# Spreading c by a VectorE shuffle instead of a TensorE product, with x squared on other engines

## The chip, the core and the metric

One core of a Trainium2 chip runs the whole program; seven cores are idle. The metric is the device time of one execution in microseconds (us), lower is better. The kernel before took 355.51 us (median of three runs, 355.11 to 355.52).

## What is computed

One layer of a hybrid model on 256 tokens of width 1024: an adaptive norm of x, a wide projection, block attention, a chunked mLSTM, a gated sum and an output projection. Only its head matters here:

```python
ada = c @ w_ada + b_ada
shift, scale, gate = jnp.split(ada[:, None, :], 3, axis=-1)
h = _rmsnorm(x, norm_w) * (1 + scale) + shift
... = jnp.split(h @ w_in, SPLIT_IDX, axis=-1)
```

c is one row of 1024 numbers. Every channel of `shift` and `scale` is a dot product of c with one column of w_ada, and `_rmsnorm` divides each token by the root of the mean of its squares plus 1e-6.

## The kernel before, in words

TensorE (PE) needs the normed, modulated x transposed, channels on the partitions: eight tiles k = 0 to 7 of 128 channels by 256 tokens, each kept as a high part `hTh` and a low part `hTl`, since every product is made from two-part numbers in three passes. The first projection phase ("P1", lines 186 and around) multiplies them with eight slabs of `w_row`, each split into `wrh` and `wrl` by ScalarE (ACT) and VectorE (DVE). After it some 25 chunks of 512 columns go through TensorE in a ring, with attention and mLSTM work hooked in between.

The order of the work on each engine is the order of the program (a manual schedule); within P1 it is a written list of steps, `P1_STEPS`, each a letter and a number. An engine takes its instructions strictly in that order, so an instruction that waits holds up all behind it. Loads go out on two queues: SyncE's (SP) carries x in two halves, then the slabs of w_ada (`adat`) and of `w_row` by turns; ACT's own queue carries c, the small table `params` (`prm`) and the bias table `relT`.

What stands ahead of P1, the part that the change touches:

- **c to all partitions (`cb`, 128 x 1024).** c lands in one partition (`crow`, a view of the second half of `xnT`, free until the transposed x is put there). Line 224 multiplies a row of ones with it, two products of 512 columns on PE into PSUM (`pc`), and line 227 on DVE and 228 on ACT copy the two halves into `cb`. `cb` is one operand of every dot product with w_ada (step `C0`, line 138, on DVE: `Ab` and `Bb`, the scale and shift of tile 0).
- **Squares and roots.** Half t of x (`xt`, 128 tokens by 1024) is squared and summed into `ssx`: half 0 on ACT (line 225), half 1 on DVE (line 229). `rstd(t)` on GpSimd (POOL) adds epsilon (line 205) and takes the power -1/2 (line 206) into `rsx`. ACT scales a unit matrix by it into `diag` (line 233).
- **Transposes with the norm in them.** `T0`, `T1`, `T2` (line 243) multiply 128 x 128 blocks of x with `diag`, so that PSUM receives normed x transposed (`xps`). A transpose of the pair kp holds four such products, two of half 0 and two of half 1. Step `t0` (line 248, ACT) copies the first pair into `xnT`.
- **Modulation.** Step `w0` (line 170, ACT) rounds the first slab, step `H0` (lines 158 and 162, ACT) makes `hTh` and `hf` of tile 0 from `xnT`, `Ab` and `Bb`; DVE makes `wrl` (line 175) and `hTl` (line 165). Step `P0` (line 186) is the first product of P1.
- **Dummies.** `keep_clock(n)` (line 217) issues n products of the unit matrix with itself into a bank that nobody reads: two at the start (`WARM = 2`), five after the products with c (step `K5`). In the trace each 128 x 128 product of this type is two records.

POOL fills the bias table (`rel_prep`, line 268) after the roots.

Of the kernel before, what the change touches and what calls it, by code (L numbers as in the profile page):

```python
# [9 lines left out]
F32 = mybir.dt.float32  # L10
F32R = mybir.dt.float32r
AF = mybir.ActivationFunctionType
OP = mybir.AluOpType
AX = mybir.AxisListType

D = 1024
# [4 lines left out]
EPS = 1e-6  # L21
# [17 lines left out]

P1_STEPS = ("R0 R1 R2 R3 K5 T0 t0 T1 T2 C0 w0 U0 H0 G0 B0 P0 x0 z0 y0 t2 B1 t1 L1 c1 a1 w1 k1 v0 Q0 q0 n0 T3 m0 "
            + "".join(f"b{k} i{k} U{k} j{k} G{k} x{k} " + ("t3 " if k == 2 else "") + f"L2 c{k + 1} z{k} y{k} a{k + 1} "
                      f"w{k + 1} k{k + 1} v{k} e{k} " for k in range(1, 7))
            + "b7 i7 U7 j7 G7 x7 z7 y7 v7 P7 Q7 q7 N7 M7").split()
WARM = 2

KX = 248
NR = 1536 + KX + 8
# [15 lines left out]
def tile_hybrid(ctx: ExitStack, tc: tile.TileContext, x, c, params, params2, rel_t, w_row, ada_mod, ada_gate,  # L65
                w_in, w_att_proj, w_ml_proj, w_out, out):
    nc = tc.nc
# [15 lines left out]
    ident = consts.tile([128, 128], F32, name="ident")  # L83
    ones = consts.tile([128, 128], F32, name="ones")
# [9 lines left out]
    mhalf = consts.tile([128, 16], F32, name="mhalf")  # L94
    qns = consts.tile([128, 1], F32, name="qns")
    ssx = consts.tile([128, 2], F32, name="ssx")
    rsx = consts.tile([128, 2], F32, name="rsx")
# [5 lines left out]
    pp = p1.enter_context(tc.tile_pool(name="ps1", bufs=1, space=PS))  # L103

    xt = ph.tile([128, 2, D], F32, name="xt")
    xnT = ph.tile([128, KT, S], F32, name="xnT")

    for t in range(2):
        nc.sync.dma_start(xt[:, t], x2[:, t])
    crow = xnT[0:1, 4:8].rearrange("p k s -> p (k s)")  # L110
    nc.scalar.dma_start(crow, c)
    nc.scalar.dma_start(prm, params)
    nc.scalar.dma_start(relT, rel_t)
    make_identity(nc, ident)
    nc.vector.memset(ones, 1.0)
# [26 lines left out]
    def modulation_sum(k, s):  # L142
        if s:
            sums[k] = ph.tile([128, 2], F32, name="sums", bufs=2)
        nc.vector.tensor_tensor_reduce(sq[:, 1], adat[k][:, s], cb, 1.0, 0.0, OP.mult, OP.add, sums[k][:, s:s + 1])
# [54 lines left out]
    diag = ph.tile([128, 2, 128], F32, name="diag")  # L200
    sq = ph.tile([128, 2, D], F32, name="sq")
    cb = ph.tile([128, D], F32, name="cb")

    def rstd(t):
        nc.gpsimd.tensor_scalar(rsx[:, t:t + 1], ssx[:, t:t + 1], EPS, None, op0=OP.add)
        nc.gpsimd.tensor_tensor(rsx[:, t:t + 1], rsx[:, t:t + 1], mhalf[:, 0:1], op=OP.pow)


    pp.tile([128, 512], F32, name="aux1")
    pp.tile([128, 1024], F32, name="pm1")  # L210
# [4 lines left out]
    def keep_clock(n):  # L215
        for _ in range(n):
            nc.tensor.matmul(pw[:, 0, 0:128], ident, ident, start=True, stop=True)  # L217

    keep_clock(WARM)


    pc = [pp.tile([128, 512], F32, name="pc0", tag="pg"), pp.tile([128, D], F32, name="pc1", tag="pm2")]
    for n in range(2):
        nc.tensor.matmul(pc[n][:, 0:512], ones[0:1, :], crow[:, n * 512:(n + 1) * 512], start=True, stop=True)  # L224
    nc.scalar.activation(sq[:, 0], xt[:, 0], AF.Square, scale=1.0 / 32, accum_out=ssx[:, 0:1])
    rstd(0)
    nc.vector.tensor_copy(cb[:, 0:512], pc[0])
    nc.scalar.copy(cb[:, 512:D], pc[1][:, 0:512])
    nc.vector.tensor_tensor_reduce(sq[:, 1], xt[:, 1], xt[:, 1], 1.0 / D, 0.0, OP.mult, OP.add, ssx[:, 1:2])
    rstd(1)  # L230
    nc.vector.scalar_tensor_tensor(b1, prm[:, P_SC:P_SC + 8], 1.0, prm[:, P_NW:P_NW + 8], op0=OP.add, op1=OP.mult)
    for t in range(2):
        nc.scalar.activation(diag[:, t], ident, AF.Copy, scale=rsx[:, t:t + 1])

    xps = {}

    def x_transposes(kp):
        pa = pp.tile([128, 2, 256], F32, name="xps", tag=("pm1", "aux1", "pg", "aux1")[kp])
        for t in range(2):
            for kk in range(2):  # L240
                k = 2 * kp + kk
                o, v = pa[:, kk, t * 128:(t + 1) * 128], xt[:, t, k * 128:(k + 1) * 128]
                nc.tensor.matmul(o, v, diag[:, t], start=t == 0 and kk == 0, stop=t == 1 and kk == 1,  # L243
                                 skip_group_check=True)
        xps[kp] = pa
# [12 lines left out]
    def some(*what):  # L258
        return lambda k: [mm_row(k, ch, (i,)) for ch, i in what]
# [18 lines left out]

    for step in P1_STEPS:
        op, k = step[0], int(step[1])  # L280
        if op == "L":
            next_loads(k)
        else:
            dict(C=modulation, H=modulate, R=rel_prep, K=keep_clock, T=x_transposes, t=x_copy, B=open_banks,
                 w=lambda k: split_hi(k, 0, 512), x=lambda k: split_hi(k, 512, 1024), y=lambda k: split_hi(k, 1024, NR),
                 U=lambda k: split_low(k, nc.vector, 0, 512), z=lambda k: split_low(k, nc.vector, 512, 1024),
                 v=lambda k: split_low(k, nc.vector, 1024, NR), G=modulate_low,
                 c=lambda k: modulation_sum(k, 1), k=lambda k: modulation_sum(k, 0),
                 a=modulation_scale, b=modulation_shift, i=lambda k: modulate(k, "i"), j=lambda k: modulate(k, "j"),
                 P=lambda k: mm_row(k, 0), Q=lambda k: mm_row(k, 1, (0, 1)), q=lambda k: mm_row(k, 1, (2,)),  # L290
                 N=lambda k: mm_row(k, 2), M=lambda k: mm_row(k, 3),
                 n=some((2, 0), (2, 1), (3, 0), (3, 1)), m=some((2, 2), (3, 2)),
                 e=some((0, 0), (0, 1), (0, 2), (1, 0), (1, 1), (1, 2), (2, 0), (2, 1), (3, 0), (3, 1), (2, 2), (3, 2))
                 )[op](k)
# [28 lines left out]
    def done(name, half):  # L323
        return 4 * (C[name, half] + 1)
# [517 lines left out]
    for nm in ("qm", "km"):  # L842
        for hf in range(2):
            s = done(nm, hf)
# [6 lines left out]
    s = done("km", 0)  # L851
    at(s + 3, ml_scores, 0)
    at(s + 4, ml_scores, 1)
    s = done("km", 1)
# [4 lines left out]
    for q, nm in enumerate(GSEG):  # L859
        s = 4 * C[nm, 0] - 4  # L860
# [5 lines left out]
    for hp in range(2):  # L866
        s = done("om", hp)
# [29 lines left out]
    for g in range(NG):  # L897
        ci, kp = divmod(g, 4)
# [4 lines left out]
        if kp == 0:  # L903
            if ci > 0:
                pc = chunks[ci - 1]
# [22 lines left out]
        for kk in range(2):  # L928
            k = 2 * kp + kk
# [74 lines left out]
```

## Time and profile before

| what | value |
|---|---|
| median of three runs | 355.51 us (355.11 to 355.52) |
| the profiled execution's own time | 354.88 us |
| its span, first to last instruction | 353.1 us |
| busy: PE, PE weight loads, DVE, ACT, POOL | 348.1, 318.9, 238.4, 212.7, 77.7 us |
| PE's share of the chain that ended last | 99% |
| first product of P1 starts | 12.15 us |
| moved by DMA | 77.95 MB, mean 221 GB/s |

Rows of a timeline begin with the start and the length in us, then the engine, the line, the operation and the tiles, output first. PEld is PE's weight load; a name ending in q (ACTq, SPq) is the engine's sequencer issuing a transfer. Square brackets hold the engine's idle time before the instruction and what ended it. Merged rows (x10) cover several instructions. In groups by line the numbers behind the bar are busy us and the mean ns of one.

### The profile page before, as it was taken

The page shows a single profiled execution, that of the slowest core. Times are in us where ns is not written, and L with a number is a line of the kernel's source. Part 1 is how long each engine was busy: PE and PEld are TensorE (multiplying, and loading weights), DVE is VectorE, ACT ScalarE, POOL GpSimd, SP SyncE. Part 2 cuts the span into 40 slices and gives each one's busy share as a digit, 9 for nine tenths or more (in the row PEclk, how much of TensorE's full clock was granted, in tenths as well). Part 3 has the DMA queues.
Part 4 walks back from the last instruction along what each step waited for, and adds up shares of the span by engine and source line. Part 5 has one row for each costly group of instructions (what it writes and reads, how often), then busy time and mean ns, then how long its engine had stood idle before and what let it go on. Part 6 is the DMA issues. An engine that isn't in the chain of part 4 may idle for free.

```text
span 353.1 us, 5961 instructions
## 1 busy us (share of the span) xinstructions
PE 348.1 (99%) x2346; PEld 318.9 (90%) x2346; DVE 238.4 (68%) x362; ACT 212.7 (60%) x329; POOL 77.7 (22%) x89
## 2 busy tenths in 40 slices
PE   8999999999999999999999999999999999999995
PEld 5888889888999999999999888888899999999885
DVE  4799988879855528767774474764475775447773
ACT  3777799898786876674654435545646374534320
POOL 4920006583005043555240000000010320000000
PEclk9999999999999999999999999999999999999999
DMA  8999999994780463493664956749219129290011
GB/s 309 417 419 420 413 375 348 212 283 194 245 291 5 127 232 124 141 384 129 238 239 132 380 204 213 265 150 381 64 28 373 78 74 376 89 358 1 2 59 59
DMA packets 24573, 77.95 MB, mean 221 GB/s; under 512 B 2909, under 2 KB 5985, under 8 KB 24034
## 3 DMA queue, kind: packets, MB, share of 16 engines
q1 hardware_dynamic: 24240, 77.03, 61.2%
q10 hardware_dynamic: 306, 0.55, 0.5%
q8 instruction: 18, 0.29, 0.3%
q14 instruction: 9, 0.07, 0.1%
HBM read 76.12 MB, written 1.45 MB: 220 GB/s over the span
## 4 chain that ended last, share of the span: by engine, by line
PE 99%; DVE 0%; POOL 0%; issue 0%; POOLq 0%
PE mm L944 15%; PE mm L942 15%; PE mm L945 14%; PE mm L937 10%; PE mm L935 10%; PE mm L936 10%; PE pm L186 9%; PE pg L186 2%; PE xps L243 1%; PE pc L224 1%; PE mm L956 1%; PE mm L954 1%; PE aux L617 1%; PE warm L217 1%; PE mm L955 1%; PE aux L467 1%
## 5 line engine op out<-in xcount | busy, mean ns | idle before, releaser
L427 DVE TENSOR_TENSOR wl<-raw,wh 128x1024 fp32r<-128x1024 f32 (+1 forms) x92 | 112.5, 1234 | 66.9 <-ACT wh L423 66.9
L423 ACT CAST wh<-raw 128x1024 fp32r<-128x1024 f32 (+1 forms) x100 | 101.9, 1031 | 58.1 <-PE mm L937 29.7
L942 PE MATMUL mm<-hTh,wh 128*128 128x256 f32 x320 | 90.1, 282 | 0.0
L945 PE MATMUL mm<-hTh,wl 128*128 128x256 f32 x320 | 88.8, 278 | 0.0
L944 PE MATMUL mm<-hTl,wh 128*128 128x256 f32 x320 | 88.8, 278 | 0.0
L942 PEld LDWEIGHTS mm<-hTh,wh 128*128 128x128 f32 x320 | 60.4, 189 | 0.0
L944 PEld LDWEIGHTS mm<-hTl,wh 128*128 128x128 f32 x320 | 60.2, 188 | 0.0
L945 PEld LDWEIGHTS mm<-hTh,wl 128*128 128x128 f32 x320 | 60.1, 188 | 0.0
L935 PE MATMUL mm<-wh,hTh 128*128 128x512 f32 (+1 forms) x144 | 55.0, 382 | 0.0
L937 PE MATMUL mm<-wh,hTl 128*128 128x512 f32 (+1 forms) x144 | 54.4, 378 | 0.0
L936 PE MATMUL mm<-wl,hTh 128*128 128x512 f32 (+1 forms) x144 | 54.3, 377 | 0.0
L937 PEld LDWEIGHTS mm<-wh,hTl 128*128 128x128 f32 x144 | 27.0, 188 | 5.0
L936 PEld LDWEIGHTS mm<-wl,hTh 128*128 128x128 f32 x144 | 27.1, 188 | 4.7
L935 PEld LDWEIGHTS mm<-wh,hTh 128*128 128x128 f32 x144 | 27.0, 188 | 4.7
L427 POOL TENSOR_TENSOR wl<-raw,wh 128x1024 fp32r<-128x1024 f32 x8 | 19.6, 2463 | 17.9 <-ACT wh L423 12.6
L757 POOL TENSOR_SCALAR f<-f 128x4 f32<-128x4 f32 x2 | 0.4, 199 | 86.8 <-DVE f L756 86.8
L175 DVE TENSOR_TENSOR wrl<-raw,wrh 128x512 fp32r<-128x512 f32 (+1 forms) x24 | 18.0, 775 | 2.0 <-ACT wrh L170 1.7
L942 PE MATMUL mm<-yah,wh 128*128 128x256 f32 x64 | 18.0, 281 | 0.0
L944 PE MATMUL mm<-yal,wh 128*128 128x256 f32 x64 | 17.7, 277 | 0.0
L945 PE MATMUL mm<-yah,wl 128*128 128x256 f32 x64 | 17.7, 277 | 0.0
L942 PE MATMUL mm<-ymh,wh 128*128 128x256 f32 x64 | 17.7, 276 | 0.0
L944 PE MATMUL mm<-yml,wh 128*128 128x256 f32 x64 | 17.7, 276 | 0.0
(210 smaller groups left out, 648.9 us busy)
## 6 DMA issues: line engine op xcount, KB each, us to landing
raw<-in_w_in_dram SPq DMA_DIRECT2D x36, 1024.0 KB, 5.1
adat<-in_ada_mod_dram SPq DMA_DIRECT2D x16, 512.0 KB, 9.4
raw<-in_ada_gate_dram SPq DMA_DIRECT2D x4, 1024.0 KB, 5.7
raw<-in_w_att_proj_dram SPq DMA_DIRECT2D x4, 1024.0 KB, 7.5
raw<-in_w_ml_proj_dram SPq DMA_DIRECT2D x4, 1024.0 KB, 8.2
raw<-in_w_out_dram SPq DMA_DIRECT2D x4, 1024.0 KB, 5.6
raw<-in_w_row_dram SPq DMA_DIRECT2D x4, 896.0 KB, 12.3
raw<-in_w_row_dram SPq DMA_DIRECT2D x4, 640.0 KB
```

Source lines behind the costliest of these rows:

```text
L175: e.tensor_tensor(l[:, cs], wrow[k][:, cs], h[:, cs].bitcast(F32), op=OP.subtract)
L186: nc.tensor.matmul(pm[ch][:, t], a[:, k, t * 128:(t + 1) * 128], b[:, cs], start=k == 0 and i == 0 and (ch < 3 or t == 0), stop=k == KT - ...
L217: nc.tensor.matmul(pw[:, 0, 0:128], ident, ident, start=True, stop=True)
L224: nc.tensor.matmul(pc[n][:, 0:512], ones[0:1, :], crow[:, n * 512:(n + 1) * 512], start=True, stop=True)
L423: nc.scalar.copy(h, w)
L427: e.tensor_tensor(l, w, h.bitcast(F32), op=OP.subtract)
L935: nc.tensor.matmul(o, a, wh[:, kk], start=first, stop=False)
L936: nc.tensor.matmul(o, a, wl[:, kk], start=False, stop=False)
L937: nc.tensor.matmul(o, b, wh[:, kk], start=False, stop=last)
L942: nc.tensor.matmul(o, wh[:, kk, cs], sh_[:, k], start=first and i % 2 == 0, stop=False, skip_group_check=True)
L944: nc.tensor.matmul(o, wh[:, kk, cs], sl_[:, k], start=False, stop=False, skip_group_check=True)
L945: nc.tensor.matmul(o, wl[:, kk, cs], sh_[:, k], start=False, stop=last and i % 2 == 1, skip_group_check=True)
```

## The change

- c is read into four partitions, 0, 32, 64 and 96, by one transfer of 4 x 1024. Since the shuffle reads all partitions, `crow` is now the whole width and is cleared first on DVE; the transfer waits for that and so goes out behind `prm`.
- DVE fills `cb` with one `stream_shuffle`, which gives every partition of a group of 32 the group's first one. The two products of line 224 and the two copies are gone.
- x's half 0 is squared on DVE, behind the shuffle, with epsilon as the sum's start, so that POOL takes its root without an addition; half 1 is squared on ACT, and POOL adds its epsilon.
- `diag` of half 0 is made on DVE, that of half 1 on ACT.
- Twelve dummies at the start in place of two, none in step `K5`, and two between the first transposes of half 0 and of half 1.

```diff
-P1_STEPS = ("R0 R1 R2 R3 K5 T0 t0 T1 T2 C0 w0 U0 H0 G0 B0 P0 x0 z0 y0 t2 B1 t1 L1 c1 a1 w1 k1 v0 Q0 q0 n0 T3 m0 "
+P1_STEPS = ("R0 R1 R2 R3 T0 t0 T1 T2 C0 w0 U0 H0 G0 B0 P0 x0 z0 y0 t2 B1 t1 L1 c1 a1 w1 k1 v0 Q0 q0 n0 T3 m0 "
...
-WARM = 2
+WARM = 12
...
-    crow = xnT[0:1, 4:8].rearrange("p k s -> p (k s)")
-    nc.scalar.dma_start(crow, c)
+    crow = xnT[:, 4:8].rearrange("p k s -> p (k s)")
+    nc.vector.memset(crow, 0.0)
     nc.scalar.dma_start(prm, params)
+    nc.scalar.dma_start(crow.rearrange("(g q) n -> g q n", q=32)[:, 0],
+                        bass.AP(tensor=c.tensor, offset=c.offset, ap=[[0, 4], [1, D]]))
     nc.scalar.dma_start(relT, rel_t)
...
-    def rstd(t):
-        nc.gpsimd.tensor_scalar(rsx[:, t:t + 1], ssx[:, t:t + 1], EPS, None, op0=OP.add)
-        nc.gpsimd.tensor_tensor(rsx[:, t:t + 1], rsx[:, t:t + 1], mhalf[:, 0:1], op=OP.pow)
...
-    pc = [pp.tile([128, 512], F32, name="pc0", tag="pg"), pp.tile([128, D], F32, name="pc1", tag="pm2")]
-    for n in range(2):
-        nc.tensor.matmul(pc[n][:, 0:512], ones[0:1, :], crow[:, n * 512:(n + 1) * 512], start=True, stop=True)
-    nc.scalar.activation(sq[:, 0], xt[:, 0], AF.Square, scale=1.0 / 32, accum_out=ssx[:, 0:1])
-    rstd(0)
-    nc.vector.tensor_copy(cb[:, 0:512], pc[0])
-    nc.scalar.copy(cb[:, 512:D], pc[1][:, 0:512])
-    nc.vector.tensor_tensor_reduce(sq[:, 1], xt[:, 1], xt[:, 1], 1.0 / D, 0.0, OP.mult, OP.add, ssx[:, 1:2])
-    rstd(1)
+    nc.vector.stream_shuffle(cb, crow, [0] * 32)
+
+    def root(t):
+        nc.gpsimd.tensor_tensor(rsx[:, t:t + 1], ssx[:, t:t + 1], mhalf[:, 0:1], op=OP.pow)
+
+    nc.vector.tensor_tensor_reduce(sq[:, 0], xt[:, 0], xt[:, 0], 1.0 / D, EPS, OP.mult, OP.add, ssx[:, 0:1])
+    root(0)
+    nc.scalar.activation(sq[:, 1], xt[:, 1], AF.Square, scale=1.0 / 32, accum_out=ssx[:, 1:2])
+    nc.gpsimd.tensor_scalar(ssx[:, 1:2], ssx[:, 1:2], EPS, None, op0=OP.add)
+    root(1)
     nc.vector.scalar_tensor_tensor(b1, prm[:, P_SC:P_SC + 8], 1.0, prm[:, P_NW:P_NW + 8], op0=OP.add, op1=OP.mult)
-    for t in range(2):
-        nc.scalar.activation(diag[:, t], ident, AF.Copy, scale=rsx[:, t:t + 1])
+    nc.vector.tensor_scalar(diag[:, 0], ident, rsx[:, 0:1], None, op0=OP.mult)
+    nc.scalar.activation(diag[:, 1], ident, AF.Copy, scale=rsx[:, 1:2])
...
         for t in range(2):
+            if kp == 0 and t == 1:
+                keep_clock(2)
```

On DVE the program begins like this before, from the first instruction to the dot products of tile 0 (the rows named ISA are the squares and dot products, each with the reading of its sum behind it):

```order
L115 MEMSET ones 128x128
L116 MEMSET mhalf 128x16
L227 COPY cb<-pc_122 128x512
L229 ISA sq,ssx<-xt 128x1024
L229 ISA ssx 128x1
L231 SCALAR_TENSOR_TENSOR b_75<-prm 128x8
L138 ISA sq,Ab<-adat,cb,b_75,prm 128x1024
```

and like this after; the clearing of `crow` is the row that writes `xnT`:

```order
L111 MEMSET xnT 128x1024
L117 MEMSET ones 128x128
L118 MEMSET mhalf 128x16
L220 STREAM_SHUFFLE cb<-xnT 128x1024
L225 ISA sq,ssx<-xt 128x1024
L225 ISA ssx 128x1
L230 SCALAR_TENSOR_TENSOR b_75<-prm 128x8
L231 TENSOR_SCALAR diag<-ident,rsx 128x128
L140 ISA sq,Ab<-adat,cb,b_75,prm 128x1024
```

The clearing, the shuffle and one `diag` have come in, and the square now belongs to x's half 0 and stands behind the shuffle.

On PE, from the first instruction to the first product of P1, before:

```order
L217 MATMUL warm<-ident 128x128 x2
L224 MATMUL pc_122<-xnT,ones 128x512
L224 MATMUL pc_123<-xnT,ones 128x512
L217 MATMUL warm<-ident 128x128 x5
L243 MATMUL xps<-diag,xt 128x128 x12
L186 MATMUL pm_200<-wrh,hTh 128x512 x2
```

and after:

```order
L215 MATMUL warm<-ident 128x128 x12
L244 MATMUL xps<-diag,xt 128x128 x2
L215 MATMUL warm<-ident 128x128 x2
L244 MATMUL xps<-diag,xt 128x128 x10
L188 MATMUL pm_202<-wrh,hTh 128x512 x2
```

The products with c are gone from PE, the dummies stand in one block ahead of the transposes, and two more part the first two transposes from the ten others.

## The prediction

> **What bounds the kernel now.** I read the page's chain of waits first, then the busy time by stretches, then TensorE's waits, and last the timeline of the first 12 us. The chain:
>
> ```profile
> PE 99%; DVE 0%; POOL 0%; issue 0%; POOLq 0%
> ```
>
> The stretches (length, then busy us and instructions of PE, weight loads, DVE, ACT, POOL, then clock, DMA share, GB/s), and what the weight loads waited for from 12 us on:
>
> ```profile
> 12.15:60.00 47.85, 47.85 (x261) 41.51 (x261) 44.88 (x71) 40.33 (x72) 12.12 (x21) 1.00 1.03 398
> 60.00:200.00 140.00, 140.00 (x1054) 133.07 (x1053) 96.16 (x170) 97.80 (x154) 50.24 (x34) 1.00 0.63 208
> 200.00:340.00 140.00, 140.00 (x929) 128.04 (x928) 87.46 (x105) 69.11 (x95) 7.71 (x8) 1.00 0.48 176
> ...
> PEld pm L186 <- DVE hTl L165: 0.2, 1, 0.2
> PEld aux L562 <- issue: 0.2, 1, 0.2
> ```
>
> From 12.15 to 340 us PE is busy without a gap; its waits come to 0.4 us. So the kernel is a head of 12.15 us and then a PE that never stops. Nothing in the change touches what comes behind the head, so the time moves by what the first product of P1 moves, one for one. The head, engine by engine:
>
> ```profile
> 4.09 1.06 ACT L225 ACTIVATE sq<-xt 128x1024 f32<-128x1024 f32 x1 [0.75 <-DMA xt<-in_x_dram]
> 5.32 0.24 POOL L205 TENSOR_SCALAR rsx<-ssx 128x1 f32<-128x1 f32 x1 [3.67 <-ACT sq L225]
> 5.65 1.47 POOL L206 TENSOR_TENSOR rsx<-rsx,mhalf 128x1 f32<-128x1 f32 x1
> 7.20 0.22 POOL L205 TENSOR_SCALAR rsx<-ssx 128x1 f32<-128x1 f32 x1
> 7.50 1.50 POOL L206 TENSOR_TENSOR rsx<-rsx,mhalf 128x1 f32<-128x1 f32 x1
> 9.03 0.40 ACT L233 ACTIVATE diag<-ident,rsx 128x128 f32<-128x128 f32 x1 [1.49 <-POOL rsx L206]
> 8.35 0.97 PEld L243 LDWEIGHTS xps<-diag,xt 128*128 128x128 f32 x4
> 9.48 2.57 PEld L243 LDWEIGHTS xps<-diag,xt 128*128 128x128 f32 x20 [0.16 <-ACT diag L233]
> 10.50 0.59 ACT L248 COPY xnT<-xps 128x512 f32<-128x512 f32 x1 [1.06 <-PE xps L243]
> 11.50 0.60 ACT L158 ACTIVATE hTh<-xnT,Bb,Ab 128x256 fp32r<-128x256 f32 x1
> 12.15 0.30 PEld L186 LDWEIGHTS pm<-wrh,hTh 128*128 128x128 f32 x2
> ```
>
> The reader is to see one chain: x's half 0 lands (4.09), is squared, POOL takes the two roots one behind the other (5.32 to 9.00), the second makes the last `diag` (9.43), which lets the remaining transposes go (9.48); the copy follows at 10.50, `hTh` at 11.50, P1 at 12.15. The chain of waits lists PE here, since dummies and products with c keep it busy, but those don't set the end: the weight loads at 9.48 waited for `diag`. POOL's first root sets the pace; whatever delays the first square delays P1.
>
> **The change, part by part.** *The products with c go.* They were off this chain, so removing them gains nothing by itself.
>
> *c's transfer is later.* It now waits for the clearing of 128 x 1024 on DVE:
>
> ```profile
> L115 DVE MEMSET ones<- 128x128 f32 x1 | 0.2, 165 | 0.8 <-PEq L991 0.8
> L116 DVE MEMSET mhalf<- 128x16 f32 x1 | 0.1, 72 | 0.0
> 0.73 0.52 ACTq L111 DMA_DIRECT2D xnT<-in_c_dram  x1
> 1.28 0.37 ACTq L112 DMA_DIRECT2D prm<-in_params_dram  x1
> 1.64 0.94 SPq L125 DMA_DIRECT2D adat<-in_ada_mod_dram  x2
> 2.56 0.49 PEld L224 LDWEIGHTS pc<-xnT,ones 1*128 1x128 f32 x2 [0.28 <-issue]
> prm<-in_params_dram ACTq DMA_DIRECT2D x1, 16.0 KB, 4.3
> ```
>
> Two clearings differ by 112 columns and 93 ns, 0.83 ns a column, so 1024 take 0.07 + 1008 x 0.83 ns = 0.91 us. DVE starts at 0.8, so c goes out at about 1.8 instead of 0.73; `prm`, now first on ACT's queue, is issued by 1.25 and holds nothing up, and `relT` and ACT's table load behind the waiting transfer have time.
>
> When does it land? The lower bound is its own lag of before: issued at 0.73, used at 2.56, thus 1.8 us, when nothing was ahead of it: 3.6. The upper bound is `prm`'s 4.3 us from issue to landing: 6.1. What lies between is the DMA traffic by queue in two stretches, 1.6 to 3.8 and 3.8 to 5.2 us (q1 is SP's, q10 ACT's; packets, MB):
>
> ```profile
> q1 hardware_dynamic: 176, 0.66, 90.8%
> q10 hardware_dynamic: 2, 0.00, 1.5%
> ...
> q1 hardware_dynamic: 144, 0.52, 97.2%
> q10 hardware_dynamic: 160, 0.02, 8.8%
> ```
>
> `prm` was issued at 1.28, but until 3.8 q10 moved two packets, which are c's. By then SP's queue had moved 0.66 MB, x's half 0 (0.52) and a bit more. So `prm` stood behind what SP had issued before it, and then ran alongside half 1. c at 1.8 would stand behind both halves (1.05 MB) and beside the first slab of w_ada (1.64). At the second stretch's 0.52 MB in 1.4 us, the missing 0.39 MB take 1.05 us: c's packets start at 4.85, and with 0.35 us for the transfer and its notice c is there at **5.2**. I take that, nearer `prm`'s row than c's own, since c now shares `prm`'s lot. Both ends stay for the range.
>
> *The shuffle stands ahead of the square on DVE*, which waits with it. No row shows a shuffle; the nearest:
>
> ```profile
> 4.67 0.69 DVE L227 COPY cb<-pc 128x512 f32<-128x512 f32 x1 [3.65 <-PE pc L224]
> 5.45 1.23 DVE L229 CUSTOM_DVE_ANT_0 sq<-xt 128x1024 f32<-128x1024 f32 x1
> 7.21 1.34 DVE L138 CUSTOM_DVE_ANT_0 sq<-adat,cb,b 128x1024 f32<-128x1024 f32 x1 [0.45 <-DMA adat<-in_ada_mod_dram]
> 9.81 0.08 DVE L138 DVE_READ_ACCUMULATOR2_ANT Bb<- 128x1 f32 x1
> ```
>
> Bounds: 0.91 (the clearing of that size) and 1.4 (two copies of 512); I take 1.2, the square's row. Shuffle 5.25 to 6.45, square of half 0 6.5 to 7.7.
>
> *POOL.* The first root needs no addition and starts 0.1 behind the square, at 7.8 (before: 5.65): 7.8 + 1.47 = 9.27. Then the addition (gap 0.08, and 0.30 to the next start) and the second root: 9.65 + 1.50 = 11.15. ACT has squared half 1 long before: DVE read that half at 5.45 without a wait, ACT needs 1.06 + 0.18. `diag` of half 1: 11.2 to 11.6; the transposes of half 1 start at 11.63 instead of 9.48, **2.15 later**. `diag` of half 0 on DVE costs 0.17 to 0.40 (a clearing of that size, ACT's row) and is done by 9.6; its two transposes and two dummies fit before 11.63. DVE waits for POOL there, and behind it stand the dot products of tile 0: 7.21 to 9.89 before, 2.7 us, so 9.6 to 12.3, while `hTh` needs them at 13.4: no cost, 1.1 us to spare.
>
> *Dummies.* The clock column reads 1.00 everywhere, so I read the clock from weight loads of one shape, dummies and later transposes:
>
> ```profile
> 1.35 0.93 PEld L217 LDWEIGHTS warm<-ident 128*128 128x128 f32 x4 [1.35 <-POOL ident masks.py:199]
> 6.26 2.21 PEld L217 LDWEIGHTS warm<-ident 128*128 128x128 f32 x10 [1.50 <-issue]
> 16.30 0.98 PEld L243 LDWEIGHTS xps<-diag,xt 128*128 128x128 f32 x8
> ```
>
> Ten in 2.21 us are one each 0.21 us; eight in 0.98 one each 0.113. The twenty at 9.48 took 2.57, against 19 x 0.113 + 0.19 = 2.34 at the quick pace, so three were still slow. Twelve dummies (24 loads) run from 1.35 to at most 6.4 and should have PE quick before the transposes: **0.23 off**.
>
> *SP's queue.* Two of its loads wait for other transfers than before: the rest of `w_row`'s first slab for `prm` instead of c (issued about 4 rather than 3.2), one half of the second w_ada slab for c instead of `prm`:
>
> ```profile
> SPq L125 <- DMA prm<-in_params_dram: 1.2, 1, 1.2
> 4.00:6.00 2.00, 2.00 (x3) 0.33 (x1) 1.24 (x2) 1.15 (x2) 0.59 (x2) 1.00 1.05 398
> ```
>
> What was issued by 3 us, 2.3 MB, fills the engines at that 398 GB/s until over 7 us, so no gap opens; c at 5.2 is no later than `prm` was, at 1.28 + 4.3 = 5.6.
>
> **Sum.** 2.15 - 0.23 = 1.92 us later. On the profiled execution's own 354.88 (span 353.1 and 1.78 around it) 356.8; on the median, 0.63 above that execution, 357.4. I can't tell how much of the 0.63 is scatter and give **357.2**. Its own range: c at 4.6 (0.6 less) to 6.1 (0.9 more), shuffle 0.2 to either side: 356.4 to 358.3.
>
> **The rivals.** *c slips past the queue: no change.* The one mechanism is the order of DMA packets. If four packets of 4 KB on ACT's queue don't stand behind SP's megabytes, c lands 1.8 us after its issue, at 3.6, 1.6 earlier: 357.2 - 1.6 = 355.6, not slower. It decides at c's landing: each us earlier is one us, and the time is over 0.2% above 355.51 (356.22) only if c lands after about 4.2. Against it is `prm`'s idle 2.5 us, a row of this very queue; for it, that c is four packets and `prm` 128. The Trainium skill ("DMA: Bandwidth & Descriptors", "Queues, rings and completion order") says that each DMA engine takes packets from its queues in turn; by that rule c would be next after the packet in progress, and the time this rival's. The trace shows turns only from 3.8 us on, not for `prm`'s first 2.5 us.
>
> *Faster.* If c lands by 2.8, the square starts with x's landing at 4.09 and the first root at 5.41 instead of 5.65: 0.24 + 0.23 = 0.47 less, and with the early dummies up to 0.5 more where a run before had its clock rise late: 354.5. It needs c in 1.0 us after issue; no row shows less than 1.8.
>
> *The clock falls back.* The dummies end by 6.4, the first transposes come at 9.6. If PE is slow again there, the twenty loads behind 11.63 take 0.21 each, 4.2 instead of 2.3 us, 1.9 more and some slow products after: 359.1 or over. For it: three idle us where before the row at 6.26 led straight into the transposes. Against it: no row shows a fall-back. The Trainium skill ("TensorE: Matmul & The Clock Gate", "Part 1: The HAM clock gate") has the clock go back to half after an idle window of about 3.4 us in a grid that runs freely; a gap of 3.2 us would not hold a whole one, but stands close.
>
> **How the numbers follow.** Forecast 0.63, no change 0.18, faster 0.06, clock 0.13. The range 355.2 to 358.6 leaves out the last two. About 0.2% (0.7 us) is what a measurement here tells from nothing: slower 0.63 + 0.13 = 0.76, same 0.18, faster 0.06.
>
> **What would show it.** Right: in the new timeline the shuffle waits for c until about 5.2, the first root starts near 7.8, the second `diag` near 11.2, P1 near 14.1, and PE then has no gaps. Wrong: a shuffle that starts before 4.2, weight loads of 0.33 us in the transposes, or a first product of P1 before 12.9.

## The result and the profile after

The kernel after took 359.21 us (median of four runs, 358.65 to 359.73), the one before 355.51 (four runs, 355.11 to 356.25): 1.0106 times as long, 95% interval 1.0094 to 1.0118. The forecast had the sign right and the size wrong: 3.7 us slower where 1.7 was forecast, 0.6 above the range. The profiled execution took 359.73 of its own (span 357.9), 4.85 more than the profiled one of before.

TensorE's weight loads up to P1, in the timeline of after:

```profile
1.35 5.20 PEld L215 LDWEIGHTS warm<-ident 128*128 128x128 f32 x24 [1.35 <-POOL ident masks.py:199]
11.07 0.93 PEld L244 LDWEIGHTS xps<-diag,xt 128*128 128x128 f32 x4 [4.52 <-DVE diag L231]
11.88 0.97 PEld L215 LDWEIGHTS warm<-ident 128*128 128x128 f32 x4
13.20 4.05 PEld L244 LDWEIGHTS xps<-diag,xt 128*128 128x128 f32 x20 [0.35 <-ACT diag L232]
17.16 0.30 PEld L188 LDWEIGHTS pm<-wrh,hTh 128*128 128x128 f32 x2
```

P1 starts at 17.16 instead of 12.15, 5.01 later, and the own time is 4.85 longer: the loss lies in the head. The twenty loads behind the second `diag` start 3.72 later than before (9.48) and take 4.05 instead of 2.57. Ahead of the first four loads (11.07) PE is idle for 4.52 us.

VectorE, of the same timeline:

```profile
1.01 0.91 DVE L111 MEMSET xnT<- 128x1024 f32 x1 [1.01 <-PEq L992]
...
7.61 0.01 DVE L220 LOAD_MASK_SELECT cb<-xnT  x1 [5.52 <-DMA xnT<-in_c_dram]
7.64 1.29 DVE L220 STREAM_SHUFFLE cb<-xnT 128x1024 f32<-128x1024 f32 x1
8.83 1.21 DVE L225 CUSTOM_DVE_ANT_0 sq<-xt 128x1024 f32<-128x1024 f32 x1
...
10.93 1.34 DVE L140 CUSTOM_DVE_ANT_0 sq<-adat,cb,b 128x1024 f32<-128x1024 f32 x1
```

DVE waits 5.52 us for c. The LOAD_MASK_SELECT belongs to the shuffle, so its start is the time at which c is there: 7.6. GpSimd, which makes the roots:

```profile
10.13 0.56 POOL L223 TENSOR_TENSOR rsx<-ssx,mhalf 128x1 f32<-128x1 f32 x1 [8.47 <-DVE b L230]
10.78 0.33 POOL L228 TENSOR_SCALAR ssx<-ssx 128x1 f32<-128x1 f32 x1
11.19 1.53 POOL L223 TENSOR_TENSOR rsx<-ssx,mhalf 128x1 f32<-128x1 f32 x1
```

The same power -1/2 of 128 numbers takes 0.56 us once and 1.53 the other time. The stretches of after in 2 us each (columns as in the prediction; the clock is the third figure from the end):

```profile
8.00:10.00 2.00, 0.00 (x0) 0.00 (x0) 2.00 (x4) 0.00 (x0) 0.00 (x0) 1.00 1.02 410
10.00:12.00 2.00, 0.93 (x4) 0.93 (x5) 1.39 (x5) 0.00 (x0) 1.70 (x3) 0.51 1.02 418
14.00:16.00 2.00, 2.00 (x11) 2.00 (x11) 0.41 (x1) 1.54 (x4) 2.00 (x15) 0.50 1.02 420
16.00:18.00 2.00, 2.00 (x13) 1.87 (x13) 1.62 (x4) 2.00 (x5) 2.00 (x8) 0.78 1.04 420
```

At about 10 us, after PE's idle stretch, the granted clock falls to a half and stays there until within 16 to 18. From 18 on it reads as before.

Three things thus differ from the forecast: c comes 2.4 us later than the 5.2 forecast, the transposes run at half clock, and one power is 0.91 cheaper. The experiments ask for the cause of each.

### The profile page after: what moved, and what is told of

Its sections match the earlier page's. It is cut to its first block, busy times and chain, and to the rows that moved or that the text cites. A ratio compares the mean times of both kernels' runs of the same rounds, so it can differ in the third digit from the quotient of the medians.

```text
span 357.9 us, 5980 instructions
## 1 busy us (share of the span) xinstructions
PE 348.7 (97%) x2356; PEld 322.1 (90%) x2356; DVE 240.1 (67%) x365; ACT 211.5 (59%) x327; POOL 75.3 (21%) x88
## 3 DMA queue, kind: packets, MB, share of 16 engines
HBM read 76.13 MB, written 1.45 MB: 217 GB/s over the span
## 4 chain that ended last, share of the span: by engine, by line
PE 95%; DMA 2%; DVE 1%; POOL 1%; issue 0%; ACT 0%; DVEq 0%
PE mm L946 14%; PE mm L945 14%; PE mm L943 14%; PE mm L936 10%; PE mm L937 10%; PE mm L938 10%; PE pm L188 9%; PE pg L188 2%; DMA xnT<-in_c_dram 2%; PE xps L244 1%; PE mm L957 1%; PE mm L955 1%; PE mm L956 1%; PE aux L618 1%; PE aux L468 1%; PE aux L580 1%
```

## The experiments

All medians are set beside runs of the kernel before on the same chip, 355.34 to 355.45 us. "P1" is the start of its first product in the profiled execution.

**1. More dummies, until the transposes.** If the slow transposes come from PE's idle stretch, dummies through it bring the clock back and nothing else moves.

```diff
-WARM = 12
+WARM = 32
```

> The changed kernel with 32 dummies at the start in place of 12, so that TensorE is never idle before the transposes. Theory (the clock fell to half because TensorE stood idle from 6.5 to 11.1 us): the transposes after the second diag run at the quick pace, 2.3 us for their twenty weight loads instead of 4.05, the first product of P1 comes near 15.5 instead of 17.2, and the time is 357.5, 1.7 below 359.2. Rival (the slow transposes come from something other than the idle time, say from what DVE or the DMA do then): 359.2, no change.

Measured: 358.10 us (357.91 to 358.31), ratio 1.0072 (1.0048 to 1.0096). The loads of this kernel:

```profile
13.10 2.31 PEld L244 LDWEIGHTS xps<-diag,xt 128*128 128x128 f32 x20 [0.74 <-ACT diag L232]
15.50 0.30 PEld L188 LDWEIGHTS pm<-wrh,hTh 128*128 128x128 f32 x2
```

The twenty loads start where they did (13.10 against 13.20) and take 2.31 instead of 4.05; P1 comes 1.66 earlier and the own time is 1.64 shorter (358.09). P1 is where I expected it, but the median fell by 1.1 us and not by 1.7. The clock's fall is shown to cost about 1.6 us between these two executions; what it cost in the others, which left no trace, stays open. What is left to before, 2.65 us, is not the clock.

**2. c ahead of the slabs of w_ada, on SP's queue.** If c stands behind what SP has issued, it comes earlier when it is issued ahead of the slabs, although no earlier in time.

```diff
-    nc.scalar.dma_start(crow.rearrange("(g q) n -> g q n", q=32)[:, 0],
+    nc.sync.dma_start(crow.rearrange("(g q) n -> g q n", q=32)[:, 0],
```

> The changed kernel with c's transfer on SP's queue, between x and the first slab of w_ada, still waiting for the clearing. Theory (c stood in the DMA engines' queue behind the first slab of w_ada, issued 0.3 us before it): c lands near 5.4 instead of 7.55, all that follows is 2.1 us earlier, 357.1 if the clock still falls back and 355.4 if the shorter idle time spares it. Rival (a transfer into four partitions is slow by itself, its issue alone takes 1.1 us): c lands at 7 or later and the time stays at 359.

Measured: 358.03 us (357.25 to 359.26), ratio 1.0072 (1.0046 to 1.0097). In the trace of this kernel c's issue, its arrival and the transposes:

```profile
1.95 0.67 SPq L113 DMA_DIRECT2D xnT<-in_c_dram  x1
...
6.08 0.01 DVE L220 LOAD_MASK_SELECT cb<-xnT  x1 [3.98 <-DMA xnT<-in_c_dram]
...
11.67 2.97 PEld L244 LDWEIGHTS xps<-diag,xt 128*128 128x128 f32 x20 [0.45 <-ACT diag L232]
```

Issued at 1.95, as in after (1.96), c is there at 6.08 instead of 7.61. So the moment of issue alone doesn't decide. The place in the order has changed, and the queue with it; this run doesn't tell the two apart. c still comes 0.7 later than I expected, and the clock falls here too: PE idles 3.1 us ahead of the transposes. For that case I had expected 357.1, which the profiled execution meets (357.25) and the median misses by 0.9.

**3. c issued 0.5 us earlier, the clearing shared by DVE and POOL.**

```diff
-    nc.vector.memset(crow, 0.0)
+    nc.vector.memset(crow[:, 0:512], 0.0)
+    nc.gpsimd.memset(crow[:, 512:1024], 0.0)
```

> The changed kernel with the clearing shared: DVE clears half of c's columns, POOL the other half, so that ACT can issue c's transfer near 1.5 us, ahead of the first slab of w_ada (1.64) instead of behind it (1.96). Nothing else differs. Theory (the DMA engines serve what was issued first, so 0.4 us of issue time are worth a slab of 0.5 MB): c lands near 6.0 instead of 7.4, and the time is near that with c ahead of w_ada, 358.0. Rival (c's landing follows its own issue by the same 5.4 us): 6.9, 358.7.

Measured: 359.51 us (359.13 to 359.86), ratio 1.0118 (1.0101 to 1.0135): no better than after. This kernel's issue, arrival, loads and clock (lines are one further down):

```profile
1.49 1.09 ACTq L114 DMA_DIRECT2D xnT<-in_c_dram  x1
...
6.69 0.01 DVE L221 LOAD_MASK_SELECT cb<-xnT  x1 [5.13 <-DMA xnT<-in_c_dram]
...
10.14 0.52 PEld L245 LDWEIGHTS xps<-diag,xt 128*128 128x128 f32 x4 [3.14 <-DVE diag L232]
12.27 4.34 PEld L245 LDWEIGHTS xps<-diag,xt 128*128 128x128 f32 x20 [1.07 <-ACT diag L233]
```

c comes 0.92 earlier, by more than the 0.47 of its issue, and the second group of transposes starts 0.93 earlier. c stayed on ACT's queue here, and its issue began 0.15 ahead of the first slab's (1.64). ACT's queue moved nothing of it before 5.6, when SP's queue had moved 1.29 MB since 1.6: c came behind x and about half of the slab, so an earlier issue spares it a part of the slab and not all. But the first four loads are quick (0.52) and the twenty behind them slow: the clock fell between the two, though PE had just worked again. It costs 0.29 more than in after, and P1 itself begins at half clock (its first two loads take 0.55 instead of 0.30). P1 starts at 16.49, 0.67 earlier than in after, and the own time (359.76) is no shorter. My 358.0 missed: c came at 6.7 and not at 6.0, and I took its gain for the kernel's.

**4. c straight to 128 partitions, without clearing and shuffle.** ACT's queue reads c 128 times, 0.5 MB, issued at 0.73.

```diff
-    nc.vector.memset(crow, 0.0)
...
-    nc.scalar.dma_start(crow.rearrange("(g q) n -> g q n", q=32)[:, 0],
...
+    nc.scalar.dma_start(cb, bass.AP(tensor=c.tensor, offset=c.offset, ap=[[0, 128], [1, D]]))
...
-    nc.vector.stream_shuffle(cb, crow, [0] * 32)
```

> The changed kernel without clearing and shuffle: c goes to all 128 partitions by one transfer of 0.5 MB on ACT's queue at 0.73. Theory (the head is then free of the late c, first product of P1 near 12, but 0.5 MB more go through the DMA engines, 1.25 us, and P1 waits for its slabs): 356.2. Rival (P1 is not held by the stream): as the version with the shuffle last, 355.0. If c's traffic in front of x costs the head more than thought, P1 starts after 13 and the time is over 357.

Measured: 358.34 us (357.8 to 358.67), ratio 1.0086 (1.0071 to 1.0101). The traffic by queue of this kernel from 1.6 to 3.8 us, and its first square:

```profile
q1 hardware_dynamic: 77, 0.32, 56.9%
q10 hardware_dynamic: 47, 0.19, 21.5%
...
6.03 1.22 DVE L222 CUSTOM_DVE_ANT_0 sq<-xt 128x1024 f32<-128x1024 f32 x1 [5.01 <-DMA xt<-in_x_dram]
```

and its loads, with the stretch that holds the clock's 0.50:

```profile
8.40 0.52 PEld L241 LDWEIGHTS xps<-diag,xt 128*128 128x128 f32 x4 [1.92 <-DVE diag L228]
11.40 4.34 PEld L241 LDWEIGHTS xps<-diag,xt 128*128 128x128 f32 x20 [2.03 <-ACT diag L229]
...
10.00:12.00 2.00, 0.59 (x3) 0.59 (x3) 1.78 (x4) 0.40 (x1) 2.00 (x4) 0.50 1.02 422
```

Issued at the same moment, the two queues share: c takes a part of x's time, x's half 0 comes at 6.0, and the head is late by x instead of c. The clock falls again: the first four loads are quick, the twenty take 4.34. The figures 356.2 and 355.0 are missed; what occurred is the case named beside them, c's traffic holding up x (P1 at 15.63), and with it the clock's fall, which I hadn't counted there.

**5. The shuffle behind the norm.** In after everything on DVE stands behind c. Here only the dot products do, which need it.

```diff
-    nc.vector.stream_shuffle(cb, crow, [0] * 32)
...
     nc.vector.tensor_scalar(diag[:, 0], ident, rsx[:, 0:1], None, op0=OP.mult)
+    nc.vector.stream_shuffle(cb, crow, [0] * 32)
```

> The changed kernel with the shuffle moved on DVE behind the square of half 0 and behind diag of half 0. Theory (c's late landing costs time because DVE is held by the shuffle in front of the square): the first root starts near 5.4, the last transposes near 9, the shuffle still waits for c until 7.6 and tile 0's dot products end near 11.6, so the first product of P1 comes near 12.3 and the time is 355.5, 3.7 below 359.2; about the time of the kernel before. Rival (c's lateness gates P1 through the dot products just as well, or the new work on DVE is what costs): 358 or more.

Measured: 355.03 us (354.87 to 355.73), ratio 0.9986 (0.9970 to 1.0002): the whole loss is gone, as expected (355.5). Roots, c's arrival and PE of this kernel:

```profile
5.69 0.56 POOL L222 TENSOR_TENSOR rsx<-ssx,mhalf 128x1 f32<-128x1 f32 x1 [4.04 <-DVE b L229]
7.19 0.58 POOL L222 TENSOR_TENSOR rsx<-ssx,mhalf 128x1 f32<-128x1 f32 x1
...
7.48 0.01 DVE L231 LOAD_MASK_SELECT cb<-xnT  x1 [0.90 <-DMA xnT<-in_c_dram]
...
8.26 2.31 PEld L244 LDWEIGHTS xps<-diag,xt 128*128 128x128 f32 x20 [0.67 <-ACT diag L232]
12.40 0.30 PEld L188 LDWEIGHTS pm<-wrh,hTh 128*128 128x128 f32 x2 [1.83 <-ACT hTh L160]
```

c is as late as in after (7.48), but the norm doesn't wait for it. The second group of transposes goes at 8.26, 1.22 earlier than before (9.48), since both powers take 0.6 us; their loads are quick, as PE idles 1.0 us ahead of the first and 0.7 ahead of these. Now `hTh`, which waits for c's dot products, is last: PE waits 1.83 us for it, and P1 starts at 12.40, 0.25 later than before. So the order on DVE made the loss; the slow second power and the fallen clock of after came with it and are gone with it.

**6. The epsilon of half 1 on DVE.** My theory for the 1.53 us of the second power was a switch of operation on POOL between addition and power. Without an addition on POOL both powers should be short. On DVE the addition stands behind `b1`, which moves ahead of it.

```diff
-    nc.gpsimd.tensor_scalar(ssx[:, 1:2], ssx[:, 1:2], EPS, None, op0=OP.add)
+    nc.vector.scalar_tensor_tensor(b1, prm[:, P_SC:P_SC + 8], 1.0, prm[:, P_NW:P_NW + 8], op0=OP.add, op1=OP.mult)
+    nc.vector.tensor_scalar(ssx[:, 1:2], ssx[:, 1:2], EPS, None, op0=OP.add)
     root(1)
-    nc.vector.scalar_tensor_tensor(b1, prm[:, P_SC:P_SC + 8], 1.0, prm[:, P_NW:P_NW + 8], op0=OP.add, op1=OP.mult)
```

> The changed kernel with the addition of epsilon for half 1 moved from POOL to DVE, so that POOL runs its two powers one behind the other. Theory (a power takes 1.5 us where another kind of operation ran just before it on POOL, and 0.56 else): the second power takes 0.56, the last diag comes 1.35 us earlier, 357.8. Rival (0.56 came from POOL's long wait before it, and a power in a row costs 1.5): only the addition and its gap go, 0.45 earlier, 358.8.

Measured: 358.87 us (358.44 to 359.17), ratio 1.0092 (1.0067 to 1.0117). POOL and PE of this kernel:

```profile
9.96 1.10 POOL L223 TENSOR_TENSOR rsx<-ssx,mhalf 128x1 f32<-128x1 f32 x2 [8.30 <-DVE b L228]
...
12.55 3.37 PEld L244 LDWEIGHTS xps<-diag,xt 128*128 128x128 f32 x20
15.85 0.30 PEld L188 LDWEIGHTS pm<-wrh,hTh 128*128 128x128 f32 x2
```

Both powers are short, so the rival falls although its 358.8 is met; and the theory falls by experiment 5, where the second power follows an addition directly and takes 0.58. P1 is 1.31 earlier here in the profiled execution, and the own time (358.44) is 1.29 shorter. Only 0.65 of it is the earlier start of the twenty loads, which stand behind eight slow ones; 0.68 is their shorter time (3.37 against 4.05), since the clock is up again within 14.5 to 15.0 here and within 16.5 to 17.0 in after. The median fell by 0.3 only; the other executions left no trace, and why they gained less stays open.

**7 and 8. What makes POOL slow.** The long powers have in common that a square or dot product, with two inputs from SBUF, begins on DVE ahead of them. So, in the order of experiment 5, an operation whose result nobody uses was put ahead of the shuffle, where POOL does its second root: once with two such inputs, once a clearing without any.

```diff
+    nc.vector.tensor_tensor(sq[:, 0], xt[:, 0], xt[:, 0], op=OP.mult)   # in 7
+    nc.vector.memset(sq[:, 0], 0.0)                                     # in 8
     nc.vector.stream_shuffle(cb, crow, [0] * 32)
```

> The version with the shuffle last, and one more product of 128 x 1024 numbers from SBUF with themselves on DVE, ahead of the shuffle, whose result nobody uses; it runs while POOL takes its second root. Theory (POOL's power stands still while DVE runs an operation with two inputs from SBUF, and ends 0.45 behind it): POOL's second addition or power grows to 1 us or more and the root ends near 8.4 instead of 7.8. Rival (what costs is another kind of operation just before on POOL): addition and power stay at 0.24 and 0.58, the root ends at 7.8.

> As the one before, with a clearing of 128 x 1024 numbers on DVE, which reads nothing, in place of the product. Both theories: addition and power keep 0.24 to 0.33 and 0.58 and the second root ends near 7.8; only if any work of DVE disturbs POOL does it grow to 1 us or more.

One run each, 355.01 and 355.30 us, looked at for POOL only. With two inputs:

```profile
6.30 1.22 DVE L231 TENSOR_TENSOR sq<-xt 128x1024 f32<-128x1024 f32 x1
...
6.75 0.86 POOL L227 TENSOR_SCALAR ssx<-ssx 128x1 f32<-128x1 f32 x1 [0.69 <-ACT sq L226]
```

and with the clearing:

```profile
6.41 0.91 DVE L231 MEMSET sq<- 128x1024 f32 x1 [0.16 <-DVE diag L230]
...
6.50 0.24 POOL L227 TENSOR_SCALAR ssx<-ssx 128x1 f32<-128x1 f32 x1 [0.57 <-ACT sq L226]
```

The addition takes 0.24 beside the clearing and 0.86 beside the operation with two inputs; it ends 0.09 behind that one (7.61 against 7.52). The power behind it takes 0.58 and ends at 8.27, near the 8.4 expected. The long powers fit: those of before end at 7.12 and 9.00, 0.44 and 0.45 behind DVE's square (6.68) and first dot product (8.55), that of after at 12.72, 0.45 behind the dot product (12.27). By this POOL stood still until DVE was done: the addition shows it, in one run of each kind, and the powers fit it by the same distance each time.

**9. Both repairs, order unchanged**: 32 dummies, epsilon on DVE.

```diff
+WARM = 32
...
-    nc.gpsimd.tensor_scalar(ssx[:, 1:2], ssx[:, 1:2], EPS, None, op0=OP.add)
+    nc.vector.scalar_tensor_tensor(b1, prm[:, P_SC:P_SC + 8], 1.0, prm[:, P_NW:P_NW + 8], op0=OP.add, op1=OP.mult)
+    nc.vector.tensor_scalar(ssx[:, 1:2], ssx[:, 1:2], EPS, None, op0=OP.add)
     root(1)
-    nc.vector.scalar_tensor_tensor(b1, prm[:, P_SC:P_SC + 8], 1.0, prm[:, P_NW:P_NW + 8], op0=OP.add, op1=OP.mult)
```

> The changed kernel with 32 dummies and with epsilon of half 1 added on DVE. Theory (the earlier second power was worth 1.6 us, but the slow TensorE swallowed it): with TensorE quick the last diag near 11.1 lets the transposes go at once, the first product of P1 comes near 14, 1.5 before that with 32 dummies alone, 356.6. Rival (P1 hangs on the dot products of tile 0, which end at 13.4, as soon as the transposes are early): first product near 14.1 too, so what tells them apart is who hTh waits for, diag's transposes or Bb. Third possibility (the power's place is worth nothing): 358.1.

Measured: 356.71 us (356.52 to 357.42), ratio 1.0039 (1.0026 to 1.0053), as expected. The loads of this kernel and the second `diag`:

```profile
10.79 0.40 ACT L232 ACTIVATE diag<-ident,rsx 128x128 f32<-128x128 f32 x1 [4.32 <-POOL rsx L223]
...
11.30 0.53 PEld L244 LDWEIGHTS xps<-diag,xt 128*128 128x128 f32 x4
...
12.20 2.31 PEld L244 LDWEIGHTS xps<-diag,xt 128*128 128x128 f32 x20
14.61 0.30 PEld L188 LDWEIGHTS pm<-wrh,hTh 128*128 128x128 f32 x2
```

With the clock up, the shorter power now shows, though c, too, came 0.35 earlier here than in experiment 1 (7.12 against 7.47). 1.3 us are still missing to before (355.39). c is one reason. The dummies are another: the loads at 11.30 show no idle time ahead of them, and the twenty go at 12.20, although the second `diag` was done at 11.19. Here 32 dummies last too long and hold the work up by a us.

**10. c on SP ahead of the slabs, and the square ahead of the shuffle.** Experiments 2 and 5 together; `diag` of half 0 stays behind the shuffle, so that the dot products follow at once.

```diff
-    nc.scalar.dma_start(crow.rearrange("(g q) n -> g q n", q=32)[:, 0],
+    nc.sync.dma_start(crow.rearrange("(g q) n -> g q n", q=32)[:, 0],
...
-    nc.vector.stream_shuffle(cb, crow, [0] * 32)
...
     nc.vector.scalar_tensor_tensor(b1, prm[:, P_SC:P_SC + 8], 1.0, prm[:, P_NW:P_NW + 8], op0=OP.add, op1=OP.mult)
+    nc.vector.stream_shuffle(cb, crow, [0] * 32)
     nc.vector.tensor_scalar(diag[:, 0], ident, rsx[:, 0:1], None, op0=OP.mult)
```

> Both remedies in the changed kernel: c's transfer on SP's queue ahead of the w_ada slabs, and on DVE the square of half 0 ahead of the shuffle, diag of half 0 behind it. Theory (P1 then hangs on c through shuffle and dot products alone: c at 6.0, shuffle to 7.4, diag, dot products 7.7 to 10.4, first product of P1 near 11.1): about 1.3 below the version with the shuffle last, 353.8, and 1.5 below the kernel before. Rival (the second power or the transposes of half 1 are late next, or the w_ada slabs, now issued 0.8 later, hold the dot products): P1 at 12 or later, 354.8 or more.

Measured: 355.11 us (354.89 to 355.39), ratio 0.9992 (0.9983 to 1.0001): 1.3 us above what I expected, level with before. PE of this kernel:

```profile
10.85 0.30 PEld L188 LDWEIGHTS pm<-wrh,hTh 128*128 128x128 f32 x2 [0.27 <-ACT hTh L160]
...
24.34 0.30 PEld L188 LDWEIGHTS pm<-wrl,hTh 128*128 128x128 f32 x2 [0.80 <-DVE wrl L177]
...
34.58 0.30 PEld L188 LDWEIGHTS pm<-wrl,hTh 128*128 128x128 f32 x2 [0.52 <-DVE wrl L177]
...
51.83 0.19 PEld L937 LDWEIGHTS mm<-wl,hTh 128*128 128x128 f32 x1
```

The same product of before, `wl` by `hTh`:

```profile
51.76 0.19 PEld L936 LDWEIGHTS mm<-wl,hTh 128*128 128x128 f32 x1
```

P1 starts 1.30 earlier than before (12.15) and ends no earlier: PE waits within it for rounded slabs (`wrl`), 0.80 and 0.52, which is what it had gained. The first of them stood on DVE behind a dot product that waited 0.78 us for its slab of w_ada (22.45), the second behind a slab of `w_row` that ACT waited for:

```profile
30.37 0.62 ACT L172 CAST wrh<-raw 128x512 fp32r<-128x512 f32 x1 [1.46 <-DMA raw<-in_w_row_dram]
```

**11 and 12. Is it the transfers?** Tile 1 takes tile 0's slabs of w_ada, so that 1 MB less is loaded ahead of P1's end; the scale and shift of tile 1 are then computed from wrong columns. Number 11 does this to the kernel of 10, number 12 to the kernel before.

```diff
     def load_ada(k):
+        if k == 1:
+            adat[1] = adat[0]
+            return
```

> The version with both remedies, without the load of tile 1's slabs of w_ada (1 MB; tile 1 takes those of tile 0, which is not what is to be computed). Theory (with P1's first product at 10.9 the DMA stream is what P1 waits for next, which swallowed the 1.3 us): the waits for wrl within P1 go, and the time comes down by the 1.3 us, 353.8. Rival (the gain went elsewhere, on PE or behind P1): 355.1.

> The kernel before without the same load of 1 MB, as the control. Theory (its PE has no gap from 12.15 us on, so its DMA stream does not bind): 355.4, no change. Rival (the stream binds it too): up to 2 us lower.

Measured: 353.86 us (353.75 to 355.54), ratio 0.9963 (0.9952 to 0.9975), for 11, and 355.02 (354.51 to 355.52), ratio 0.9990 (0.9980 to 0.9999), for 12. Set against before on the same chip, 10 is 0.28 us lower and 11 is 1.48: one MB less brings 1.2 us where the head is short and 0.3 where it is that of before. So what swallowed the early start in 10 is the stream of transfers, of which the kernel before feels only some 0.3. The trace of 11 can't show the waits closed: in its profiled execution, the longest (355.54), the clock fell, and P1 started only at 12.59.

One more variant wasn't tried: c into four partitions at 0.73 without the clearing. The shuffle would read partitions that nothing has written.

## Why the prediction was right and wrong

**What bounds the kernel: right in the direction of slower.** Start of P1 and own time moved together in after (5.01 and 4.85) and between after and experiment 1 (1.66 and 1.64). Own time less P1's start is 342.6 to 343.3 us in all profiled executions but that of 10, where it is 344.07. So downwards "one for one" doesn't hold: 1.30 earlier brought nothing there. The quoted stretch from 12.15 to 60 had a DMA share of 1.03, which I read only for gaps.

**c's landing: the step that failed.** "c at 1.8 would stand behind both halves and beside the first slab of w_ada", with 6.1 as upper bound; it was there at 7.6. c's issue was right (1.96, and the clearing 0.91 as worked out). Its place was not. The traffic of SP's queue (q1) in after from 1.6 to 3.8, 3.8 to 5.2 and 5.2 to 7.0 us, and of ACT's (q10) from 1.6 to 3.8, 5.2 to 6.2 and 6.2 to 7.0:

```profile
q1 hardware_dynamic: 181, 0.68, 88.7%
...
q1 hardware_dynamic: 142, 0.52, 101.2%
...
q1 hardware_dynamic: 183, 0.69, 96.5%
...
q10 hardware_dynamic: 144, 0.02, 5.1%
...
q10 hardware_dynamic: 2, 0.01, 2.0%
...
q10 hardware_dynamic: 17, 0.01, 4.5%
```

ACT's queue moved nothing from 3.8 to 5.2. The 144 packets are `prm`'s and a few small ones: `prm`, now first on its queue at 0.73, went alongside x. c's four packets of 4 KB came only behind 5.2, about two by 6.2 and the rest after, and DVE had the notice at 7.6. From 1.6 to 5.2 SP's queue had moved 1.20 MB; at 0.69 in 1.8 us it had moved about 1.58 by 6.2, which is both halves of x (1.05) and the whole first slab (0.52), issued from 1.64 on, 0.3 ahead of c. So c stood behind the slab, not beside it. Experiment 2 agrees: ahead of the slabs at the same moment of issue, though on SP's queue, c came 1.5 earlier. Why packets of one queue stand behind those of another stays open. `prm`'s lag of before, 4.3 us, was no upper bound, since `prm` had only x ahead of it. The 0.35 us for transfer and notice had no row behind it: c's first two packets came between 6.1 and 6.2, 1.3 later than the 4.85 forecast, and from there to the notice it took some 1.45 us, so this term was 1.1 too small. The step's size in all: +2.36.

**The shuffle and square: right.** 7.61 to 10.04, 2.43 us, against 2.45.

**POOL: mis-sized.** I gave the first power the 1.47 us of before as its own time. It is 0.56 when no DVE operation with two inputs from SBUF began ahead of it: −0.91. (7 and 8 show the same of the addition.) In before the square of half 1 ran on DVE at that moment, and the change took it away; the second power stays slow beside the dot product. The pause from the first power's end to the second's was 2.03 instead of 1.88: +0.15.

The Trainium skill ("SBUF — State Buffer", "Who interferes with whom") says that a DVE instruction with two inputs in SBUF contends with a GpSimd instruction that reads SBUF, that the shared ports are locked for one of them alone, and that the order of issue decides which one blocks. The trace agrees: 0.86 against 0.24 for the addition, with an end 0.09 behind DVE's.

**The dummies: wrong, and the clock rival happened.** "Should have PE quick before the transposes, 0.23 off": the twenty loads took 4.05 instead of 2.34, +1.71 (4.2 was the rival's figure). The rival had 0.13 with c at 5.2, a gap of 3.2 us; c's lateness made it 4.5. That the first error brought the second isn't shown: the clock also fell with gaps of 3.1 us (2), of 1.9 and 2.0 (4) and of 2.5 (11), so it might have fallen with c at 5.2. That the rival's 359.1 stands so near the measured 359.21 is luck in part, since it held none of the other errors that the sum below adds up.

The Trainium skill ("TensorE: Matmul & The Clock Gate", "Part 1: The HAM clock gate") lets the clock fall to half after an idle window of about 3.4 us. The trace agrees on the half (0.50). It differs on the idle window: in experiment 6 the clock fell 2.3 us into PE's idle stretch, and in experiment 4 it was down in the stretch from 10 us on although PE had idled for only 1.92 and 2.03 us with a us of products between.

**The sum.** P1 was forecast at 14.07. 14.07 + 2.36 − 0.02 − 0.91 + 0.15 + 1.71 leaves 17.36; measured is 17.16. The last 0.20 is at the end of the transposes, whose row ends 0.09 behind P1's start (17.25), where before it ended 0.10 ahead (12.05). This accounts for the profiled execution, whose own time was forecast at 356.8 and measured at 359.73. The median missed by less, 2.0 us: it lies 0.5 below the profiled execution, where I had put it 0.4 above, and no trace shows what the other executions had less of.

**The other points.** `diag` of half 0 and the dot products cost nothing, as said: the last of them ended at 13.6, the copy that `hTh` needs began at 14.46. SP's queue left no gap from 8 us on, DMA share 1.02 and more, although it waited 1.9 us for c (half of the second w_ada slab), which I had expected no later than before. "c slips past the queue" fell, c having waited longer than forecast, not shorter; "faster" with it.

The turn-taking of the Trainium skill ("DMA: Bandwidth & Descriptors", "Queues, rings and completion order"), named beside that rival, shows where two queues start at the same moment (0.32 and 0.19 MB in experiment 4), and not for c, issued behind 1 MB and more of others.

Nothing tried here beats the kernel before with the same computation: 355.03 (5) and 355.11 (10) are level with it, since 5 loses to c's dot products what it gains at the transposes, and 10 to the transfers what it gains at P1's start.

## What to carry to other kernels

Before an operation that waits for a late transfer is put into an engine's order, count what stands behind it: the shuffle cost 1.3 us of work, and 3.7 us of time, because x's square, both roots and all transposes queued behind its wait, and moving that one line gave it all back. A small transfer's landing is to be estimated from the bytes issued ahead of it on all queues, not from the lag of another small transfer that had less ahead of it. And dummies keep the clock only if they last until close to the work, and hold the work up if they last longer (9): when something moves the work, their number has to move too.

## What the runs showed of the hardware

- A power of 128 numbers on POOL takes 0.56 to 0.58 us alone and 1.47 to 1.66 when a DVE operation with two inputs from SBUF began shortly ahead of it; it then ends 0.44 to 0.45 behind that one. A power that began ahead of the DVE operation took 0.58 to 0.65 (12 and 10; in 6 the two took 1.10 together).
- The shuffle of 128 x 1024 took 1.29 to 1.34 us, about the time of a square.
- The clock fell between 2.2 and 4.0 us behind the last weight load of the early dummies (worked out from the clock of half-us stretches: about 7.6 in experiment 11, 7.9 in 6, 10.0 in after, 11.0 in 3), in two kernels (3 and 4) with products in between. It held with 1.0 and 0.7 us of idle (5) and 1.6 (10). Where the limit lies, and on what its moment depends, stays open.
- Why c's notice comes 0.6 us behind the last of its packets (moved by 7.0, notice at 7.6), or more, stays open.
